# A hybrid decoder layer on one core: input projection by plain products, first weight sums of the MLP moved, final norm without GpSimd

## The chip, the cores and the metric

One core of a Trainium2 chip runs the whole layer as one program. The metric is device microseconds (us) of an execution, lower is better; comparisons are made between medians of several executions. The engines are TensorE (PE: matmuls; PEld its weight loads), VectorE (DVE), ScalarE (ACT), GpSimd (POOL) and SyncE (SP), which issues most DMAs. They run side by side, each through its own list of instructions in a fixed order, and wait for one another by semaphores.

## The reference

The input `x` is 1024 tokens by 1024 features in f32. One layer does, in f32:

```
h    = rmsnorm(x)
proj = h @ w_in                      # 1024 x 3080: u, v(gate MLP), q, k, v, gate, beta, decay
y_a  = gelu(u) * (tril(W_s) @ layernorm(gelu(v)) + b_s)        # chunks of 128 tokens, 4 groups
q, k, v = silu(causal depthwise conv of width 4)               # 4 heads x 128
y_b  = rmsnorm(gated delta rule(l2norm(q), l2norm(k), v)) * silu(gate)     # chunks of 64
x    = x + concat(y_a, y_b) @ w_out
x    = x + cross attention of rmsnorm(x) on 256 memory tokens  # 4 heads x 256
x    = x + relu(rmsnorm(x) @ w1)^2 @ w2                         # width 4096
out  = rmsnorm(x)
```

## The kernel before

Activations lie transposed in SBUF: features on the 128 partitions, tokens along the free axis, as eight blocks of features by two halves of 512 tokens. Every f32 product is made of three matmuls on rounded operands: an operand is split into a rounded part (`hi`, a CAST on ACT, L133) and the rest (`lo`, a subtraction on DVE, L134), and `mm3` issues hi x hi, hi x lo and lo x hi (L154 to L156). One product of a 128-row block of weights with 512 tokens over all 1024 features is 8 x 3 = 24 matmuls 128x512.

The program runs in stages: the gate MLP's `v` (0 to 54 us), the input projection with all that follows it per head (54 to 346 us), the delta rule (to some 550 us), the output projection, the memory attention (to some 780 us), w1 and w2 of the MLP, and the final norm.

**The input projection** works on 24 blocks of 128 output features; four of them (`v` of the gate MLP) are done by then. Blocks 0 and 1 are plain products (`u_block`, L385: 48 matmuls each). The other 18 go two at a time through `pair` (L491), which forms a 2 x 2 block product with 7 products instead of 8: each of the seven is 12 matmuls (`prod`, L507). What is saved is paid for with sums: of the weights, four for each pair, on GpSimd (L525 to L528), of the activations (`comb`, L421, on GpSimd, and the split operands that `quad` makes), and of the results: a PSUM bank that two results share is copied out by ACT (`save`, L517) before PE goes on adding into it, and the copy is added when a result is taken (L592 and others on DVE). A pair needs seven weight operands, split one by one just ahead of their product.

Results are taken by rows: `URow` (gelu), `GateRow` (silu, times a gain, stored to DRAM) and `ConvRow`: a convolution of width four along the tokens, one step on ACT (L604) and three on DVE (L606), then silu on ACT (L609). What follows a ConvRow on PE, the transposes to token order (L797) and the products k k^T and q k^T (L834), is put off by `post(..., PLAG)`: it comes when the counter that `boundary` (L473) raises after each product has gone `PLAG` further. L764 sums the log decays within chunks, of operands that GpSimd makes (L755). L716 is the mixing of the gate MLP, whose operands DVE normalises (L689). L574 takes a gate's result.

**The triangular inverse** of the delta rule, 31 steps of two DVE instructions that depend on one another (`inv_steps`, L892: L896 and L899), reads a matrix that is stored to DRAM (`u_d`) and loaded back (`ub_d` into `M`). Its result goes out as `ti_d` and comes back as `Tc`, which the first PE work of the delta rule reads (L1193). Until it is there PE runs `fill` work (products of the memory's keys and values, 128x256), in portions that `FILL` sets.

**The MLP's w1** (`w1_pair`, L1700) uses the same 2 x 2 scheme; its four sums of weights are on DVE (L1785 to L1788), its operands of activations are made by `early_quads` (in the attention's last stage) and `late_quads` (L1593). **The final norm** (`Norm`, L1888) sums squares on GpSimd (L1904), sums over partitions on PE (`rms_tok`, L179, columns of one), takes square root and reciprocal, spreads the result over the partitions (`rows`, L188) and multiplies: six of eight blocks on DVE (L1922), two by ACT and GpSimd (L1919, L1920).

A scheduler of the framework sets each engine's order, starting from that of the program text; on PE, from the delta rule on, due times written into the program set it. The orders printed below are those of the built programs.

## Time and profile before

| | |
|---|---|
| runs | 1437.39, 1436.9, 1433.65 us; median 1436.9 |
| profiled execution | 1440.11 us, span of its instructions 1438.1 us |
| mean granted TensorE clock | 0.975 of full speed |
| PE busy | 1379.9 us (96%) |
| DVE, ACT, POOL busy | 1054.4 (73%), 662.4 (46%), 223.6 us (16%) |

The profile's matmuls are pipelined, so that one is shown as busy while the next has begun: the rate of starts, not the busy share, tells how full PE is. A matmul 128x512 is shown with about 0.39 us but starts come about 0.23 us apart when nothing holds it up. The granted clock is 1.0 (2.4 GHz) or 0.5 (1.2 GHz) at any time; a mean between the two says which part of a stretch ran at the lower level.

### The profile page before, as it was taken

To read this page: it belongs to the slowest core of one execution; us is meant where nothing else is said; L and a number is where in the kernel's file an instruction comes from. 1 tells how busy PE (TensorE), PEld (TensorE's weight loads), DVE (VectorE), ACT (ScalarE), POOL (GpSimd) and SP (SyncE) were. 2 spreads that over 40 slices of the span, in tenths; PEclk is the share of its full clock that TensorE was granted. 3 is DMA by queue.
4 is the path that set the end of the run, shared out by engine and by line. 5 is a ranking of instruction groups with operands and counts; after the bars stand their busy time and mean duration, and the time that the engine had idled before them with its cause. 6 is when DMAs were issued, how large, how long until landed. Compare 5 with 4: busy or idle time off the path is not lost. (4 is left out here: it accounts for less than half of the span.)

```text
span 1438.1 us, 19110 instructions
## 1 busy us (share of the span) xinstructions
PE 1379.9 (96%) x6934; PEld 1147.7 (80%) x6934; DVE 1054.4 (73%) x1711; ACT 662.4 (46%) x1164; POOL 223.6 (16%) x182
## 2 busy tenths in 40 slices
PE   9989998979999999999999899999999999999996
PEld 8777777758998888888888788787787788888885
DVE  8797877789576656855547867766668997787775
ACT  7463565647455425744325444443344334333332
POOL 7551644440111102000000000000000000000024
PEclk9998999989999999999999999999999999999996
DMA  5102244538988878221300344444448664443203
GB/s 207 44 30 84 93 123 125 161 90 282 337 288 259 282 231 269 89 67 66 118 6 10 117 161 160 134 136 142 154 161 278 256 206 146 162 137 126 73 1 118
DMA packets 137008, 213.15 MB, mean 148 GB/s; under 512 B 22609, under 2 KB 73809, under 8 KB 136914
## 3 DMA queue, kind: packets, MB, share of 16 engines
q1 hardware_dynamic: 84352, 154.69, 33.6%
q10 hardware_dynamic: 52562, 57.25, 11.7%
q8 instruction: 54, 0.88, 0.2%
q14 instruction: 40, 0.33, 0.1%
HBM read 143.74 MB, written 68.16 MB: 147 GB/s over the span
## 5 line engine op out<-in xcount | busy, mean ns | idle before, releaser
L1904 POOL TENSOR_TENSOR rB<-rB,fq 128x256 f32<-128x256 f32 (+1 forms) x18 | 18.9, 1047 | 823.8 <-ACT fq L1902 823.3
L154 PE MATMUL mm<-A,wh 128*128 128x512 f32 (+1 forms) x368 | 138.0, 375 | 6.9 <-ACT F L517 4.4
L156 PE MATMUL mm<-A,wl 128*128 128x512 f32 (+1 forms) x368 | 135.0, 367 | 0.0
L133 ACT CAST wh<-raw 128x512 fp32r<-128x512 f32 (+1 forms) x110 | 83.1, 772 | 76.7 <-PE dn L155 24.0
L134 DVE TENSOR_TENSOR wl<-raw,wh 128x512 fp32r<-128x512 f32 (+1 forms) x103 | 97.2, 948 | 17.8 <-ACT wh L133 17.0
L155 PE MATMUL mm<-B,wh 128*128 128x512 f32 x240 | 97.7, 407 | 0.0
L154 PEld LDWEIGHTS mm<-A,wh 128*128 128x128 f32 x368 | 72.5, 197 | 18.5 <-ACT F L517 5.1
L156 PEld LDWEIGHTS mm<-A,wl 128*128 128x128 f32 x368 | 72.4, 197 | 10.7 <-DVE wl L134 0.5
L133 ACT CAST sp<-rw 128x1024 fp32r<-128x1024 f32 x36 | 37.5, 1051 | 92.6 <-issue 42.0
L1785 DVE TENSOR_TENSOR F<-raw 128x512 f32<-128x512 f32 x15 | 10.4, 693 | 70.5 <-DMA raw<-in_ffn_w_dram 70.5
L155 PE MATMUL mm<-A,wh 128*128 128x256 f32 (+1 forms) x192 | 61.9, 323 | 0.0
L154 PE MATMUL mm<-sp,sp 128*128 128x512 f32 (+1 forms) x152 | 58.1, 386 | 2.1 <-DVE A L1948 2.1
L155 PE MATMUL mm<-sp,sp 128*128 128x512 f32 (+1 forms) x152 | 58.5, 385 | 1.6 <-DVE sp L134 1.6
L156 PE MATMUL mm<-sp,sp 128*128 128x512 f32 (+1 forms) x152 | 58.3, 384 | 0.0
L155 PEld LDWEIGHTS mm<-B,wh 128*128 128x128 f32 x240 | 47.5, 198 | 9.5
L134 DVE TENSOR_TENSOR sp<-rw,sp 128x1024 fp32r<-128x1024 f32 x36 | 43.8, 1218 | 14.3 <-ACT sp L133 14.3
L1880 DVE TENSOR_TENSOR A<-mm,A 128x512 f32<-128x512 f32 x64 | 43.3, 684 | 8.5 <-PE mm L156 8.3
L154 PE MATMUL mm<-E,wh 128*128 128x512 f32 x116 | 45.4, 392 | 0.0
L155 PE MATMUL mm<-E,wh 128*128 128x512 f32 x116 | 45.1, 389 | 0.0
L1752 ACT ACTIVATE F<-F 128x512 f32<-128x512 f32 x31 | 19.6, 632 | 53.8 <-DVE F L1751 53.8
L1063 DVE TENSOR_TENSOR Y<-mm,Y 128x512 f32<-128x512 f32 x32 | 22.1, 690 | 29.5 <-PE mm L156 29.3
L1880 DVE TENSOR_TENSOR A<-dn,A 128x512 f32<-128x512 f32 x48 | 32.8, 686 | 13.7 <-PE dn L156 13.1
(688 smaller groups left out, 4309.6 us busy)
## 6 DMA issues: line engine op xcount, KB each, us to landing
raw<-in_ffn_w_dram SPq DMA_DIRECT2D x32, 512.0 KB, 4.6
raw<-in_w_in_dram SPq DMA_DIRECT2D x20, 512.0 KB, 3.9
rw<-hid_T_d SPq DMA_DIRECT2D x18, 512.0 KB, 3.3
hid_T_d<-F ACTq DMA_DIRECT2D x33, 256.0 KB, 2.1
rw<-hid_B_d SPq DMA_DIRECT2D x14, 512.0 KB, 3.3
Z<-in_ffn_w_dram SPq DMA_DIRECT2D x12, 512.0 KB, 4.1
rw<-in_ffn_w_dram SPq DMA_DIRECT2D x12, 512.0 KB, 5.0
hid_B_d<-F ACTq DMA_DIRECT2D x22, 256.0 KB, 2.4
```

The lines of the kernel that those rows point to most:

```text
L133: nc.scalar.copy(hi, src)
L134: (lo_eng or nc.vector).tensor_tensor(lo, src, hi.bitcast(F32), op=ALU.subtract)
L154: nc.tensor.matmul(out, wh, xh, start=start, stop=False, skip_group_check=more)
L155: nc.tensor.matmul(out, wh, xl, start=False, stop=False, skip_group_check=more)
L156: nc.tensor.matmul(out, wl, xh, start=False, stop=stop, skip_group_check=more)
L1063: nc.vector.tensor_tensor(a, ps[:], a, op=ALU.add)
L1752: nc.scalar.activation(o, o, AF.Square)
L1785: nc.vector.tensor_tensor(s1, a21, a22, op=ALU.add)
L1880: nc.vector.tensor_tensor(acc, ps[:], acc, op=ALU.add)
L1904: nc.gpsimd.tensor_tensor(self.sa, self.sa, self.sq, op=ALU.add)
```

## The change

The projection. The 18 blocks of the pairs become 18 plain rows; with blocks 0 and 1 there are 20, in the order `ORDER`, 48 matmuls each. `fetch_block` loads raw weights three to four blocks ahead into a ring of four buffers, `split_block` splits a whole block (128x1024) two blocks ahead into a ring of three. There are no sums of weights or activations, no saved banks; the scale 1/rms, which `before` put into the activations, is multiplied into each result on DVE when it is taken. `boundary` now comes after each 12 matmuls, and `PLAG` is 4. Between them, `hook` spreads small work over the rows: the gate MLP's statistics and mixing (`todo`), from row V1 on two steps of the inverse at each of the four hooks of a row, and the memory's norm in the last two rows.

The delta rule. The two `run_fill(1)` with the inverse's remainder go (it is done in the projection); `FILL` is 0.6 instead of 0.56.

The MLP. `first_sums` loads the first two blocks of w1, splits the first and makes the four sums of pair 0 during the last of the four groups of `attention_output`. The operand T3 is made of x11 and the difference that T2 already holds, T4 of x21 and the same: for each of four blocks one ACT and one DVE instruction fewer.

The final norm. The squares are summed on DVE (18 additions), all products are on DVE, and in the last quarter `rms_rows` takes the place of `rms_tok` and `rows`.

The core of the diff (names of tiles that only move, and the class bodies that lose the argument `plus`, left out):

```diff
-PLAG = 1
+PLAG = 4
 SLAG = 1
 MS, MN = 2, 5
-LOV = (3, 4)
-INV = (16, 31)
-FILL0, FILL = 5, 0.56
+INV = 2
+FILL0, FILL = 5, 0.6
+    def rms_rows(self, dst, parts):
+
+        ps = self.dn()
+        n = dst.shape[1]
+        for i, a in enumerate(parts):
+            self.nc.tensor.matmul(ps[:, :n], self.ones, a, start=i == 0, stop=i == len(parts) - 1)
+        self.nc.scalar.activation(dst, ps[:, :n], AF.Sqrt, bias=self.eps, scale=1.0 / D)
+        self.nc.vector.reciprocal(dst, dst)
+
...
-    def pair(rows_, saves, s1_tag, hook=None, los=()):
...
-        pa = e.mm()
-        w = slot()
-        e.split_copy(w[0], w[1], raw[0], eng(0))
-        wa, wb = ([v[:, 4 * b:4 * b + 4] for v in w] for b in range(2))
-        s1 = T(s1_tag, [P, 4, P])
-        nc.gpsimd.tensor_tensor(s1, a21, a22, op=ALU.add)
-        nc.gpsimd.tensor_tensor(a21, a11, a21, op=ALU.subtract)
-        nc.gpsimd.tensor_tensor(a11, s1, a11, op=ALU.subtract)
-        nc.gpsimd.tensor_tensor(a12, a12, a11, op=ALU.subtract)
-        prod(pa, wa, "11", True)
-        p1 = save(pa)
-        w = slot()
-        w2, w1 = split(w, 0, a11, 1), split(w, 1, s1, 2)
-        pb = e.mm()
-        prod(pb, wb, "21", True)
-        rows_[0].take(0, pb, p1)
-        prod(pa, w2, "T2", False)
-        u = save(pa)
-        w = slot()
-        w3, w4 = split(w, 0, a21, 3), split(w, 1, a12, 4)
-        pc = e.mm()
-        prod(pc, w1, "T1", True)
-        p5 = save(pc)
-        w5 = T("rB", [P, 4, P], F32R), T("rB2", [P, 4, P], F32R)
-        e.split_copy(*w5, a22, eng(5))
-        fetch_pair()
-        prod(pa, w3, "T3", False)
-        rows_[1].take(1, pa, p5)
-        prod(pc, w4, "22", False)
-        rows_[0].take(1, pc, u)
-        prod(pa, w5, "T4", False)
-        rows_[1].take(0, pa, None)
+    U, Q, K, V, G = ([n + i for i in range(4)] for n in (0, 8, 12, 16, 20))
+    ORDER = (U[0], U[1], G[0], K[0], Q[0], U[2], K[1], Q[1], U[3], K[2], Q[2], G[1], K[3], Q[3],
+             V[0], V[1], G[2], V[2], V[3], G[3])
+    ahead = deque(ORDER)
+    raws, ready = deque(), deque()
+    def fetch_block():
+        if ahead:
+            n = e.ring.get("wraw", 0)
+            e.ring["wraw"] = n + 1
+            tag = ("raw", "raw", "Z4", "Z5")[n % 4]
+            r = T(tag, [P, KT, P], F32, RAW if tag == "raw" else 1)
+            nc.sync.dma_start(r, t["w_in"][ahead.popleft()])
+            raws.append(r)
+    def split_block():
+        if raws:
+            n = e.ring.get("wsplit", 0)
+            e.ring["wsplit"] = n + 1
+            w = [T(t_, [P, KT, P], F32R, 2 if t_[0] == "w" else 1)
+                 for t_ in (("wh", "wl"), ("wh", "wl"), ("Z0", "Z1"))[n % 3]]
+            e.split_copy(*w, raws.popleft())
+            ready.append(w)
+        fetch_block()
+    def row(taker, hook=None):
+        wh, wl = ready.popleft()
+        for hf in range(2):
+            ps = e.mm()
+            for k in range(KT):
+                e.mm3(ps[:], wh[:, k], wl[:, k], *X[k][hf], k == 0, k == KT - 1)
+                if k == KT // 2 - 1:
+                    if hf == 0:
+                        split_block()
+                    if hook:
+                        hook()
+                    boundary()
+            taker.take(hf, ps)
+            if hook:
+                hook()
+            boundary()
         def take(self, hf, ps):
             pre = e.R("F0 F1 C18 C19", [P, 515])
-            if plus is None:
-                nc.scalar.copy(pre[:, 3:515], ps[:])
-            else:
-                nc.vector.tensor_tensor(pre[:, 3:515], ps[:], plus, op=ALU.add)
+            nc.vector.tensor_tensor(pre[:, 3:515], ps[:], rB[hf], op=ALU.mult)
...
+    def some_inv():
+        inv_steps(min(31, done[0] + INV))
+
+    row(v_row(0))
+    M = T("E2", [P, 32, 32])
+    nc.sync.dma_start(M, ub_d)
...
+    row(v_row(1), some_inv)
+    row(GateRow(2), some_inv)
+    row(v_row(2), some_inv)
+    row(v_row(3), lambda: (some_inv(), mem_norm()))
+    row(GateRow(3), lambda: (some_inv(), mem_norm()))
...
-    for n in INV:
-        run_fill(1)
-        inv_steps(n)
     inv_steps(31)
...
         if q == "T3":
-            nc.scalar.mul(b, x22, g2)
-            nc.vector.scalar_tensor_tensor(b, x12, n1, b, op0=ALU.mult, op1=ALU.add)
+            b = e.R("xr0 xr1 B3", [P, 512])
+            nc.vector.scalar_tensor_tensor(b, x11, n1, diff[j], op0=ALU.mult, op1=ALU.add)
         else:
-            hi, lo = XQ["T2"][j]
-            nc.vector.scalar_tensor_tensor(b, x21, g2, hi.bitcast(F32), op0=ALU.mult,
-                                           op1=ALU.subtract)
-            nc.vector.tensor_tensor(b, b, lo.bitcast(F32), op=ALU.subtract)
+            b = diff[j]
+            nc.vector.scalar_tensor_tensor(b, x21, g2, b, op0=ALU.mult, op1=ALU.subtract)
         put(q, j, b)
+    def first_sums():
+        for b in range(2):
+            r = T("raw", [P, KT, P], F32, RAW)
+            nc.sync.dma_start(r, t["ffn_w1"][b])
+            first_raw.append(r)
+        a11, a12, a21, a22 = (first_raw[b][:, 4 * i:4 * i + 4] for b in range(2) for i in range(2))
+        w = [T(t_, [P, KT, P], F32R, 2) for t_ in ("wh", "wl")]
+        e.split_copy(*w, first_raw[0])
+        yield
+        s1 = T("B1", [P, 4, P])
+        nc.vector.tensor_tensor(s1, a21, a22, op=ALU.add)
+        nc.vector.tensor_tensor(a21, a11, a21, op=ALU.subtract)
+        yield
+        nc.vector.tensor_tensor(a11, s1, a11, op=ALU.subtract)
+        nc.vector.tensor_tensor(a12, a12, a11, op=ALU.subtract)
+        first_raw.extend((w, s1))
+        yield
...
-                nc.gpsimd.tensor_tensor(self.sa, self.sa, self.sq, op=ALU.add)
+                nc.vector.tensor_tensor(self.sa, self.sa, self.sq, op=ALU.add)
...
+            if n0 > 0:
+                e.rms_rows(rb, [self.sa, self.sq])
...
-                    if m in (2, 5):
-                        nc.scalar.mul(acc, acc, g_of("norm_final", m))
-                        nc.gpsimd.tensor_tensor(ob[:, b], acc, rb, op=ALU.mult)
```

How the order changes, at three places.

PE in the projection. Before, rows around the first transposes of k of head 0 (`E_264`, half 0); the product that this half is taken from, `mm_1422`, ends at row 562:

```order
588 L154 MATMUL mm_1496<-A_150_785,wh_1416 128x512
589 L155 MATMUL mm_1496<-B_151_786,wh_1416 128x512
590 L156 MATMUL mm_1496<-A_150_785,wl_1417 128x512
591 L797 MATMUL dn_1471<-ident_86,E_264_1379 128x128 x4
592 L154 MATMUL mm_1381<-A_158_815,wh_1490 128x512
593 L155 MATMUL mm_1381<-B_159_816,wh_1490 128x512
594 L156 MATMUL mm_1381<-A_158_815,wl_1491 128x512
```

After, the same transposes (`E_183`); the product they come from, `mm_989`, ends at row 410:

```order
448 L153 MATMUL mm_1089<-A_44_261,wh_903 128x512
449 L154 MATMUL mm_1089<-B_45_262,wh_903 128x512
450 L155 MATMUL mm_1089<-A_44_261,wl_904 128x512
451 L701 MATMUL dn_1109<-ident_86,E_183_988 128x128 x4
452 L153 MATMUL mm_1089<-A_55_308,wh_903 128x512
453 L154 MATMUL mm_1089<-B_56_309,wh_903 128x512
454 L155 MATMUL mm_1089<-A_55_308,wl_904 128x512
```

The transposes moved back by half a product: before, 24 matmuls 128x512 of projection products (and four others) stand between the product and the transposes of its result; after, 36 (and four others).

DVE where the inverse begins. Before, in the row pair of v1 and gate 3 (L896, L899 the inverse; L592 takes a result, L606 the convolution, L134 a split):

```order
418 L899 TENSOR_TENSOR E_495_2643<-E_495_2643,E_496_2646 128x31
419 L896 TENSOR_TENSOR E_496_2646<-E_455_2414,E_495_2643 128x60
420 L899 TENSOR_TENSOR E_495_2643<-E_495_2643,E_496_2646 128x30x2
421 L896 TENSOR_TENSOR E_496_2646<-E_455_2414,E_495_2643 128x87
422 L899 TENSOR_TENSOR E_495_2643<-E_495_2643,E_496_2646 128x29x3
423 L896 TENSOR_TENSOR E_496_2646<-E_455_2414,E_495_2643 128x112
424 L899 TENSOR_TENSOR E_495_2643<-E_495_2643,E_496_2646 128x28x4
425 L896 TENSOR_TENSOR E_496_2646<-E_455_2414,E_495_2643 128x135
```

After, in row V1 (L812, L815 the inverse; L500 takes V1's two halves from `mm_2392` and `mm_2446`; L514 the convolution):

```order
316 L812 TENSOR_TENSOR E_381_2251<-E_402_2381,E_380_2248 128x31
317 L815 TENSOR_TENSOR E_380_2248<-E_380_2248,E_381_2251 128x31
318 L812 TENSOR_TENSOR E_381_2251<-E_402_2381,E_380_2248 128x60
319 L815 TENSOR_TENSOR E_380_2248<-E_380_2248,E_381_2251 128x30x2
320 L812 TENSOR_TENSOR E_381_2251<-E_402_2381,E_380_2248 128x87
321 L815 TENSOR_TENSOR E_380_2248<-E_380_2248,E_381_2251 128x29x3
322 L812 TENSOR_TENSOR E_381_2251<-E_402_2381,E_380_2248 128x112
323 L500 TENSOR_TENSOR C_413_2433<-mm_2392,rB_440 128x512
324 L815 TENSOR_TENSOR E_380_2248<-E_380_2248,E_381_2251 128x28x4
325 L506 COPY C_418_2483<-C_413_2433 128x3
326 L812 TENSOR_TENSOR E_381_2251<-E_402_2381,E_380_2248 128x135
327 L815 TENSOR_TENSOR E_380_2248<-E_380_2248,E_381_2251 128x27x5
```

Before, the first steps of the inverse stand in one run; after, one or two stand between the steps of each convolution, and the first of them stands ahead of the taking of V1's first half.

DVE at the start of w1. Before, the sums of pair 0 (L1785 to L1788) stand among the splits of its operands, behind the attention's last result (L1624):

```order
945 L1624 TENSOR_TENSOR A_1364_6832<-dn_7370,A_1364_6832 128x512
946 L134 TENSOR_TENSOR E_1450_7517<-F_1449_7514,E_1450_7517 128x512
947 L139 SCALAR_TENSOR_TENSOR E_1467_7592<-A_1362_6828,vec_84,E_1467_7592 128x512
948 L208 TENSOR_TENSOR rB_1367_6837<-rB_1367_6837,xr_1433_7396 128x512
949 L1590 SCALAR_TENSOR_TENSOR B_1436_7404<-F_1434_7399,ng_6834,B_1436_7404 128x512
950 L1785 TENSOR_TENSOR xr_1448_7505<-raw_7469 128x512
951 L1601 SCALAR_TENSOR_TENSOR xr_1455_7532<-A_1360_6824,ng_6834,xr_1455_7532 128x512
952 L134 TENSOR_TENSOR Y_1437_7407<-B_1436_7404,Y_1437_7407 128x512
953 L1786 TENSOR_TENSOR raw_7469<-raw_7467,raw_7469 128x512
954 L134 TENSOR_TENSOR Y_1447_7504<-xr_1448_7505,Y_1446_7503 128x512
955 L1787 TENSOR_TENSOR raw_7467<-xr_1448_7505,raw_7467 128x512
```

After, the sums (L1543 to L1547) and the first split stand around the attention's results (L1569), four of which are still to come behind them:

```order
815 L1569 TENSOR_TENSOR A_1256_6609<-mm_7001,A_1256_6609 128x512
816 L1543 TENSOR_TENSOR B_1319_7082<-raw_7035 128x512
817 L1507 TENSOR_TENSOR F_1335_7197<-A_1256_6609,A_1172_6189 128x512
818 L216 TENSOR_TENSOR rB_1263_6622<-rB_1263_6622,xr_1306_7027 128x512
819 L1544 TENSOR_TENSOR raw_7035<-raw_7033,raw_7035 128x512
820 L138 SCALAR_TENSOR_TENSOR Y_1336_7199<-F_1335_7197,vec_84,Y_1336_7199 128x512
821 L1546 TENSOR_TENSOR raw_7033<-B_1319_7082,raw_7033 128x512
822 L133 TENSOR_TENSOR wl_7365<-raw_7035,wh_7364 128x512
823 L1547 TENSOR_TENSOR raw_7033<-raw_7033 128x512
824 L1569 TENSOR_TENSOR A_1257_6611<-dn_7041,A_1257_6611 128x512
```

The four sums moved ahead of the attention's last four results.

## Rows read from the trace of the kernel before

**Rows 1.** The page: busy time by engine; granted clock in 40 slices.

```profile
PE 1379.9 (96%) x6934; PEld 1147.7 (80%) x6934; DVE 1054.4 (73%) x1711; ACT 662.4 (46%) x1164; POOL 223.6 (16%) x182
PEclk9998999989999999999999999999999999999996
```

**Rows 2.** Stretches: length, busy us by engine (count), clock, DMA share, GB/s.

```profile
54.00:345.90 291.90, 262.35 (x1210) 210.30 (x1209) 241.00 (x481) 154.15 (x351) 129.86 (x100) 0.94 0.37 107
345.90:382.00 36.10, 34.63 (x297) 33.70 (x295) 24.87 (x46) 22.81 (x32) 4.62 (x5) 0.95 1.06 348
780.00:822.00 42.00, 37.96 (x165) 30.08 (x164) 34.35 (x57) 24.13 (x43) 0.00 (x0) 0.92 0.29 101
1152.00:1224.00 72.00, 72.00 (x320) 59.61 (x319) 63.70 (x68) 29.76 (x30) 0.00 (x0) 1.00 0.54 182
1400.00:1438.00 38.00, 24.00 (x145) 22.80 (x144) 21.61 (x38) 11.68 (x29) 17.18 (x20) 0.70 0.32 111
```

**Rows 3.** Waits of PE, 54 to 346 us: total us, times, longest.

```profile
PE dn L797 <- ACT E L609: 16.6, 8, 5.0
PE mm L154 <- ACT F L517: 4.4, 1, 4.4
PE mm L154 <- ACT C L517: 2.8, 3, 1.7
PE mm L154 <- DVE C L574: 2.0, 1, 2.0
PE dn L716 <- DVE C L689: 1.6, 2, 1.1
PE dn L764 <- POOL C L755: 1.6, 2, 1.1
PE dn L764 <- POOL xr L755: 0.5, 1, 0.5
```

**Rows 4.** Timeline of PE at its longest wait there: start, duration, instruction.

```profile
292.77 0.39 PE L154 MATMUL mm<-A,wh 128*128 128x512 f32 x1
298.11 1.11 PE L797 MATMUL dn<-ident,E 128*128 128x128 f32 x4 [4.95 <-ACT E L609]
```

**Rows 5.** Groups on DVE and ACT there: busy us, mean ns | idle before.

```profile
L606 DVE SCALAR_TENSOR_TENSOR F<-F,vec,F 128x512 f32<-128x512 f32 x33 | 27.5, 842 | 0.1
L134 DVE TENSOR_TENSOR wl<-raw,wh 128x1024 fp32r<-128x1024 f32 x11 | 15.1, 1373 | 4.6 <-ACT wh L133 4.5
L592 DVE TENSOR_TENSOR F<-mm,C 128x512 f32<-128x512 f32 x12 | 8.2, 685 | 4.2 <-PE mm L156 2.7 <-ACT F L604 1.4
L835 DVE TENSOR_TENSOR E<-dn,E 128x512 f32<-128x512 f32 x16 | 10.9, 680 | 0.3 <-PE dn L834 0.3
L609 ACT ACTIVATE E<-F 128x512 f32<-128x512 f32 x21 | 13.3, 635 | 15.6 <-DVE F L606 15.5
```

**Rows 6.** The inverse on DVE; the load of its matrix (KB, us).

```profile
L896 DVE TENSOR_TENSOR E<-E,E 128x31 f32<-128x31 f32 (+15 forms) x31 | 13.6, 438 | 0.7
L899 DVE TENSOR_TENSOR E<-E,E 128x31 f32<-128x31 f32 (+15 forms) x31 | 12.4, 402 | 0.7
E<-u_d SPq DMA_DIRECT2D x1, 512.0 KB, 6.2
```

**Rows 7.** Waits of PE, 345 to 382 us (delta rule's start).

```profile
PE dn L1193 <- DMA Tc<-ti_d: 0.8, 1, 0.8
```

**Rows 8.** Waits of PE, 780 to 822 us (start of w1).

```profile
PE dn L154 <- ACT wh L133: 3.0, 1, 3.0
```

**Rows 9.** The end, 1400 to 1438 us: PE's waits; DVE timeline.

```profile
PE dn L179 <- POOL rB L1904: 3.6, 1, 3.6
PE mm L154 <- DVE A L1948: 2.1, 3, 1.6
1406.41 3.56 DVE L1922 SCALAR_TENSOR_TENSOR rw<-A,vec,fr 128x512 f32<-128x512 f32 x2
```

**Rows 10.** A reciprocal on DVE (timeline, 117 us).

```profile
116.76 0.34 DVE L653 RECIPROCAL E<-E 128x32 f32<-128x32 f32 x1
```

More of the change, by code (lines that the diff above doesn't have):

```diff
@@ L313, in hybrid @@
     z = [None] * NC
+    zz = {}
     def gv_step(ps, c, k):
@@ L854, in spill, with v_row, qk_rows @@
         return run
-    for h in range(NH):
+    def v_row(h):
+        vv = T(f"E{6 + h % 2}", [P, 2, 512])
+        vT = [vv[:, hf] for hf in range(2)]
+        return ConvRow(8 + h, vT, lambda hf: v_post(h, hf, vT))
+    def qk_rows(h):
         steps_ = decays(h)
```

223 lines of the change are left out of this document (78 added, 145 removed).

## Prediction

> **What bounds the kernel now.** Read first the share of PE and the clock: PE is shown busy for 1379.9 of 1438.1 us [rows 1], so at first sight there are 58 us to win. That share misleads, since a matmul is shown as busy while it waits for the one ahead; the count of starts is the better measure. A stretch that nothing disturbs holds 320 matmuls in 72 us at the full clock, 0.225 us for each 128x512 [rows 2]. The projection (54 to 345.9 us) ran at a mean clock of 0.94 [rows 2]; with two levels, 1.0 and 0.5, a mean 0.06 below full over 291.9 us is 17.5 us of work lost (35 us at the lower level). The page's slices have their lowest clock, 0.8, at 108 and 288 us, and 0.6 in the last one [rows 1]. Next the waits of PE by what released it: 29.5 us in the projection, 16.6 of them transposes that wait for a silu of a convolution, 7.2 the first matmul of a product that waits until ACT has copied a shared PSUM bank, 2.0 DVE taking a result, 1.6 and 2.1 others [rows 3]. The timeline shows what the longest is like: a matmul starts at 292.77, the transposes behind it only at 298.11, after a silu [rows 4]. Waits and clock together are 47 us in this stretch; from 1152 to 1224 us both are nil. So PE bounds everything, and what can be won is mostly in the first 350 us, some at the start of w1 and at the end.
>
> **The change, part by part.**
>
> *Work added.* A pair is 7 products of 12 matmuls, 84; two rows are 96. Nine pairs: 9 x 12 = 108 more matmuls 128x512, 108 x 0.225 = **+24.3 us**. That is certain, and on the path, as PE bounds.
>
> *Waits and clock of the projection.* The saves go, and the weight operands are ready two blocks ahead, so 7.2 us of the waits [rows 3] lose their cause. The transposes now stand 36 matmuls behind the product they come from, not 24: 8.1 us and not 5.4, at 0.225. What must fit in between for one half: taking 0.69, three convolution steps of 0.84, a step of ACT and the silu 0.64 [rows 5], some 4.6 to 5 us with the handovers, and another 1.4 where a split of 128x1024 stands between [rows 5]. By the old distance each hiccup of DVE reaches PE, by the new one 2 to 3 us of queue are swallowed. So the question is whether DVE keeps up. A row of q: two takings 1.4, six steps 5.1, a split 1.4, four products with the decays 2.7 [rows 5], small ones near 0.5: 11.1 us; a row of k is about as long, a row of u or gate 5 to 6. PE needs 48 x 0.225 = 10.8 for a row and near 1 for its transposes and small products. A round of k, q, u is 28 of DVE against 35 of PE: DVE fits, with peaks in the q rows. GpSimd's sums fall away, so PE's two waits for GpSimd's operands (2.1 us [rows 3]) shrink; I leave 1 us of them.
>
> The rows V are the hard ones. The inverse is 62 instructions in 26.0 us [rows 6], now two steps at each of four hooks, 26.0 x 8/31 = 6.7 us in a full row: a V row holds 1.4 + 5.1 + 1.4 + 6.7 = 14.6 us of DVE against 11.8 of PE. And its first step stands ahead of the taking of V1's first half on DVE, waits for the load of the matrix, which took 6.2 us once issued [rows 6], behind a store, behind the last products of q, which themselves now come later by the new distance. I put that load's landing some 9 us behind V0's end, DVE idle for 5 to 6 us, queued behind it V1's convolution, and PE 3 to 5 us at V1's transposes; V2 can lose a further 1 to 4. The mixing, done early, has no such wait.
>
> Residue: V rows 6, hiccups in the q rows 3, GpSimd and others 1, and about 3 for the clock after two or three longer waits: **13 us** left of 47, so −34. Both ends: 5 (only the wait for the load) and 27 (V rows as they were, half of the other waits and dips).
>
> *The start of the delta rule.* The inverse ends within the V rows, so the wait for its result, 0.8 us [rows 7], and the dip that goes with 0.95 over 36.1 us, 1.8 us [rows 2], should go; the fill work is moved, not changed. **−2** (−2.6 to +1: fills run out ahead of the first chunk).
>
> *The start of w1.* It holds a wait of 3.0 us of a product on a split of the second pair's weights [rows 8] and 0.08 x 42 = 3.4 us of clock [rows 2], 6.4 in all. Pair 0's sums and first split, 4 x 0.69 + 1.4 on DVE, leave the busiest 5 us of that engine, as do four subtractions; the buffers come free that much earlier, and so does the second pair's load. **−4.5** (−6.4 to +2: the sums stand ahead of the attention's last four results on DVE, and PE would wait for those).
>
> *The end.* GpSimd's share goes: two DVE products beside it took 3.56 us [rows 9], two of them elsewhere 2 x 0.84 at most [rows 5], and PE waited 2.1 us on the additions queued behind them [rows 9]: −2. The last chain waits 3.6 us on GpSimd's sum [rows 9]; an addition 128x256 is shorter on DVE, but DVE has 18 additions and six products more. The reciprocal of 128x256 is new: 0.34 us for 32 columns [rows 10] bounds it by 0.34 x 8 = 2.7 above, half of a 512-column addition, 0.35, below [rows 5]; I take 1.5, the middle. In return four transposing products, a copy and two column sums fall. I take **−1.5** (−4 to +2). The Trainium skill ("VectorE: DVE Perf Modes", "First, the fixed hardware budget") has the reciprocal run on an iterative divider with a repeat count of 8; at its clock of 0.96 GHz that would be an estimate of 2.1 us for 256 columns. By the same rule 32 columns would be 0.27 and the row shows 0.34 [rows 10], so the trace agrees; by it the end would be −0.9 instead of −1.5.
>
> *Sum.* +24.3 − 34 − 2 − 4.5 − 1.5 = −17.7 against the profiled execution of 1440.1, so 1422.4. That execution is 3.2 above the median of 1436.9; taken from the median, **1419**.
>
> **The rivals.**
>
> *Nearly every wait goes.* The residue is 5: 8 us better, 1411, and with w1 and the end at their better ends 1407; I take **1409**. For it: DVE has 20% in hand over most rows. Against: 14.6 against 11.8 in the V rows.
>
> *The inverse turns the V rows into DVE's.* Residue 27: +14, **1433**. It decides if the matrix lands more than some 12 us behind V0's end, so that V1 and V2 both wait. For it: 62 dependent instructions in line with the convolutions, and waits of up to 5.0 us at just such a place before [rows 3]. Against: only four of 20 rows have it.
>
> *Slower: DVE becomes the bound of all k, q and v rows.* The place is the convolution on DVE; the 24.3 us of matmuls are paid while the waits stay. To be slower by over 0.3% (4.3 us, about what a measurement of this kernel can tell from no change) the residue must exceed 34 + 13 − 24.3 + 8 + 4.3 = 35 us, so 12 rows must lose some 2 to 3 us each: a q row would have to take 14 us on DVE rather than 11.1. With a residue of 41 it would be **1447**. For it: DVE is busy for 241 of 291.9 us already [rows 2], and its queue is strictly in order, with takings behind products that wait for PE. Against: the sum of a round, and the removal of the activations' operands and bank additions from DVE.
>
> *It does nothing to the rest.* If the parts behind the projection bring nothing (they are off the path), 8 us of the gain fall and 1427 is left; that lies in the forecast's own range.
>
> **How the numbers follow.** Forecast (1411 to 1429, residue 8 to 20 with the other terms at either end) 0.55; nearly all waits go 0.17; V rows on DVE 0.16; slower 0.12. The range takes in the second and third: 1405 to 1434, leaving out the slower case and tails, near 0.2. Faster by over 0.3% means below 1432.6: the forecast, the first rival and half of the V-row case, 0.80. Within: the other half of it and a little of the slower case, 0.10; slower 0.10.
>
> **What the profile after would show.** Right: some 108 matmuls more, the projection about 12 us shorter from 54 us on, waits of PE on silu under 8 us and concentrated in the V rows, no wait on a saved bank, a clock of 0.98 or more there; no wait for the inverse's result; the wait at w1's second pair gone; no GpSimd beside DVE at the end. Wrong: DVE at 95% and more over whole rows of k and q, transposes waiting at each of them, the clock again near 0.94, PE waiting for DVE's takings, or new waits of the attention's last results on DVE. The forecast falls if the residue is over 27 or if the order of DVE makes one late load hold up a chain that I have counted as hidden.

## The result, and the profile after

The changed kernel takes 1416.4 us (median of four runs, 1415.7 to 1421.9), the kernel before 1435.3 (four runs): a ratio of 0.989, 95% interval 0.986 to 0.992. The forecast was 1419, so the time came out near it. The parts did not: two gains were larger than forecast, and a loss that no term held took most of the surplus away.

The page of the kernel after: span, busy time by engine, granted clock in 40 slices (it answers to [rows 1]).

```profile
span 1414.0 us, 19001 instructions
PE 1378.4 (97%) x7034; PEld 1154.2 (82%) x7034; DVE 1002.5 (71%) x1666; ACT 617.1 (44%) x1061; POOL 107.7 (8%) x100
PEclk9999999999999999999999999999999999999997
```

A hundred matmuls more, and PE is shown busy 1.5 us less: a matmul that waits behind another counts as busy, so this share says nothing of the gain. The slices at 0.8 in the projection are gone.

The stretches tell more. Columns: stretch, length, busy us of PE, PEld, DVE, ACT and POOL (count of each), granted clock, DMA share, GB/s. I cut the span at two events that both kernels have, the first fill matmul (the projection's end) and the last products with `Yc` (the last chunk's solve in the delta rule), and at a point 38 us ahead of the end. The projection of before is in [rows 2]; its other stretches:

```profile
345.90:524.00 178.10, 176.09 (x1460) 159.93 (x1459) 118.43 (x234) 89.08 (x148) 25.95 (x22) 0.99 0.91 289
524.00:1400.00 876.00, 864.53 (x3881) 711.03 (x3877) 628.48 (x910) 368.48 (x579) 21.11 (x14) 1.00 0.40 134
```

The same four stretches after:

```profile
54.00:325.70 271.70, 268.92 (x1332) 223.31 (x1331) 192.11 (x399) 118.00 (x268) 42.45 (x43) 0.99 0.43 124
325.70:512.20 186.50, 175.80 (x1449) 158.83 (x1447) 114.99 (x215) 86.55 (x143) 25.22 (x20) 0.98 0.83 252
512.20:1376.00 863.80, 858.04 (x3873) 708.11 (x3871) 626.66 (x910) 365.28 (x573) 12.57 (x9) 1.00 0.41 136
1376.00:1414.00 38.00, 22.76 (x142) 20.69 (x140) 26.25 (x59) 9.33 (x23) 0.00 (x0) 0.75 0.32 111
```

A cut 38 us ahead of the end gives the end the same length in both kernels, so the table goes on by events from the delta rule on: the last result of the attention that DVE takes (L1624, after the change L1569), and the first and the last result that `w2_group` takes (L1880, after it L1830).

| stretch | before | after | difference | forecast |
|---|---|---|---|---|
| projection, from 54 us | 291.9 | 271.7 | −20.2 | −9.7 |
| its end to the last products with `Yc` | 178.1 | 186.5 | +8.4 | −2 |
| to the attention's last result | 255.6 | 254.5 | −1.1 | none |
| to w2's first result (w1) | 328.1 | 318.1 | −10.0 | −4.5 |
| to w2's last result | 266.0 | 265.9 | −0.1 | none |
| to the end | 64.4 | 63.3 | −1.1 | −1.5 |
| sum (one execution of each) | | | −24.1 | −17.7 |

The profiled execution of before is 4.8 us above the median of its four runs, that of after 0.7 below: the 24.1 of the traces are some 19 in the medians, and differences of a few us between two traces can be scatter.

What PE waited for after (total us, times, longest). In the projection, in place of the seven rows and 29.5 us of [rows 3]:

```profile
PE dn L701 <- ACT E L517: 2.7, 1, 2.7
```

In the delta rule, 325 to 520 us (the two longest; [rows 7] showed 0.8 at its start, a wait that is gone):

```profile
PE dn L1206 <- ACT B L1200: 5.3, 1, 5.3
PE mm L154 <- DVE wl L133: 1.8, 1, 1.8
```

At the start of w1 (767 to 809 us, against [rows 8]) and in the last 38 us (against [rows 9]):

```profile
PE mm L153 <- ACT B L1678: 0.5, 1, 0.5
...
PE dn L187 <- DVE rB L1854: 3.5, 1, 3.5
PE mm L153 <- DVE A L1897: 2.6, 3, 1.0
```

So two places are open: why the projection lost nearly all of its 47 us of waits and clock, not 34, and where the delta rule's 8.4 us come from.

**The delta rule's new wait.** The timeline of after around it (start, duration, engine, instruction, idle before and its releaser; ACTq rows are DMA issues on ACT's queue):

```profile
442.12 0.42 DVE L907 TENSOR_TENSOR A<-mm,xr 128x256 f32<-128x256 f32 x1
442.82 0.58 ACT L750 COPY xr<-dn 128x512 f32<-128x512 f32 x1
449.72 0.69 DVE L485 TENSOR_TENSOR xr<-mm,rB 128x512 f32<-128x512 f32 x1 [3.32 <-DMA vt_d<-xr]
455.38 6.69 ACTq L947 DMA_DIRECT2D vw_d<-A  x4
465.71 0.58 ACT L1200 COPY B<-dn 128x512 f32<-128x512 f32 x1 [1.57 <-issue]
466.35 2.07 PE L1206 MATMUL dn<-B,B 128*128 128x128 f32 x8 [5.29 <-ACT B L1200]
```

L907 is the last reader of `rBm`, the spread norm of the memory. L750 copies a half of V2's values, L485 takes a gate's result: both are projection work, whose matmuls ended at 325, and they run some 120 us later. They write the buffer `xr1`, and `rBm` lies in `xr1`. The change had lengthened the ring `TR`, from which the values, the gates and the operands of the log decays are taken, by that buffer; the diff has it among the tiles that only move:

```diff
-    TR = "C24 C25 xr0"
+    TR = "C24 C25 xr0 xr1"
```

My reading: a row of V2 takes `xr1` from the ring, must wait until the memory's keys are scaled at 442, and hands its lateness on: the store from `xr1` holds L485 and DVE for 3.3 us, the load of these values comes late, and stores and copies on ACT pile up ahead of L1200, which a chunk's chain needs. The experiment e_rbm settles whether this buffer is the cause; the links in between are read from this timeline alone.

**The projection's old waits.** First what ACT waited for there in the kernel before (54 to 346 us, the longest total of its list):

```profile
ACT wh L133 <- POOL raw L527: 18.1, 5, 5.7
```

An instance of it, timeline of before: GpSimd's third weight sum (L527) behind another product of its own, ACT, and the transposes on PE.

```profile
196.98 1.49 POOL L822 TENSOR_TENSOR E<-E,E 128x512 f32<-128x512 f32 x1
198.43 1.30 POOL L527 TENSOR_TENSOR raw<-C,raw 128x512 f32<-128x512 f32 x1
199.76 0.62 ACT L133 CAST wh<-raw 128x512 fp32r<-128x512 f32 x1 [3.33 <-POOL raw L527]
200.29 0.73 ACT L604 ACTIVATE F<-C,vec 128x512 f32<-128x512 f32 x1
205.20 0.63 ACT L609 ACTIVATE E<-F 128x512 f32<-128x512 f32 x1 [1.14 <-DVE F L606]
205.88 0.66 PE L797 MATMUL dn<-ident,E 128*128 128x128 f32 x4 [3.01 <-ACT E L609]
```

GpSimd's third sum ends at 199.73; the CAST that splits it stands ahead of the convolution's step L604 in ACT's queue, which is in order, so L604 starts some 3 us late, the silu follows, and PE waits 3.0 us for it. This wait, which [rows 3] put down to a silu, began with an addition on GpSimd. The two other long ones of the k and q rows, and ACT's wait for GpSimd in the same stretches (210 to 250 and 250 to 290 us):

```profile
237.32 1.01 PE L797 MATMUL dn<-ident,E 128*128 128x128 f32 x4 [2.77 <-ACT E L609]
267.96 0.66 PE L797 MATMUL dn<-ident,E 128*128 128x128 f32 x4 [1.57 <-ACT E L609]
```

```profile
ACT wh L133 <- POOL raw L527: 3.1, 1, 3.1
...
ACT wh L133 <- POOL raw L527: 2.3, 1, 2.3
```

Each time PE waits a little less than ACT did: 3.0, 2.8 and 1.6 against 3.3, 3.1 and 2.3. ACT's two other waits of the five, 3.7 and 5.7 us (they end at 118 and 153 us), are not followed by such a wait of PE, so 8.7 of the 18.1 us stand ahead of 7.3 us of silu waits. After 290 us, in the V rows, ACT has no such wait, and PE still waits three times for a silu there, at 298 [rows 4], 310 and 337, for 8.3 us together. At 298 the three convolution steps stand on DVE between splits and last 0.74, 1.21 and 1.21 us, GpSimd's additions beside them. So the 16.6 us are two parts, 7.3 and 8.3, with causes of their own (the last 0.9 are two short waits). After the change there are no weight sums that ACT could wait for.

### The profile page after: what moved, and what is told of

It reads as the page before. It is cut to its first block, busy times and chain, and to the rows that moved or that the text cites. A ratio compares the mean times of both kernels' runs of the same rounds, so it can differ in the third digit from the quotient of the medians.

```text
span 1414.0 us, 19001 instructions
## 1 busy us (share of the span) xinstructions
PE 1378.4 (97%) x7034; PEld 1154.2 (82%) x7034; DVE 1002.5 (71%) x1666; ACT 617.1 (44%) x1061; POOL 107.7 (8%) x100
## 5 line engine op out<-in xcount | busy, mean ns | idle before, releaser
L153 PE MATMUL mm<-A,wh 128*128 128x512 f32 (+1 forms) x416 | 153.6, 369 | 0.0
L155 PE MATMUL mm<-A,wl 128*128 128x512 f32 (+1 forms) x416 | 149.2, 359 | 0.0
L154 PE MATMUL mm<-B,wh 128*128 128x512 f32 x288 | 112.9, 392 | 0.0
L155 PEld LDWEIGHTS mm<-A,wl 128*128 128x128 f32 x416 | 78.9, 190 | 12.1 <-DVE wl L133 0.2
L153 PEld LDWEIGHTS mm<-A,wh 128*128 128x128 f32 x416 | 79.0, 190 | 11.1
L132 ACT CAST wh<-raw 128x512 fp32r<-128x512 f32 (+1 forms) x79 | 63.0, 808 | 56.2 <-PE dn L154 23.4
L133 DVE TENSOR_TENSOR wl<-raw,wh 128x512 fp32r<-128x512 f32 (+1 forms) x78 | 74.2, 953 | 18.4 <-ACT wh L132 17.7
L154 PEld LDWEIGHTS mm<-B,wh 128*128 128x128 f32 x288 | 54.6, 190 | 10.6
L1735 DVE TENSOR_TENSOR F<-raw 128x512 f32<-128x512 f32 x15 | 10.4, 691 | 57.6 <-DMA raw<-in_ffn_w_dram 57.6
L1830 DVE TENSOR_TENSOR A<-mm,A 128x512 f32<-128x512 f32 x64 | 43.3, 684 | 8.5 <-PE mm L155 8.3
L154 PE MATMUL mm<-B,Z 128*128 128x512 f32 x124 | 48.4, 390 | 0.0
L1830 DVE TENSOR_TENSOR A<-dn,A 128x512 f32<-128x512 f32 x48 | 32.7, 685 | 13.7 <-PE dn L155 13.1
L155 PE MATMUL mm<-E,wl 128*128 128x512 f32 x108 | 42.1, 390 | 0.0
```

Source lines behind the costliest of these rows:

```text
L132: nc.scalar.copy(hi, src)
L133: (lo_eng or nc.vector).tensor_tensor(lo, src, hi.bitcast(F32), op=ALU.subtract)
L153: nc.tensor.matmul(out, wh, xh, start=start, stop=False, skip_group_check=more)
L154: nc.tensor.matmul(out, wh, xl, start=False, stop=False, skip_group_check=more)
L155: nc.tensor.matmul(out, wl, xh, start=False, stop=stop, skip_group_check=more)
L1735: nc.vector.tensor_tensor(s1, a21, a22, op=ALU.add)
```

## Experiments

Twelve kernels, in three sets on one chip each; the kernel before was run with each set (medians 1433.3, 1434.7, 1433.1). The kernel e_rbm is the base of seven of them.

| kernel | median us | ratio to before, 95% |
|---|---|---|
| e_again: after, unaltered | 1419.6 | 0.991 (0.988 to 0.993) |
| e_rbm: after, `rBm` in a buffer of its own | 1403.7 | 0.980 (0.977 to 0.983) |
| e_mlp_old: after, MLP as before | 1424.1 | 0.993 (0.991 to 0.995) |
| e_norm_old: after, final norm as before | 1418.1 | 0.989 (0.986 to 0.992) |
| e_before_far: before, PLAG 3 | 1448.0 | 1.008 (1.006 to 1.011) |
| e_near: e_rbm, PLAG 3 | 1410.9 | 0.983 (0.981 to 0.985) |
| e_inv_late: e_rbm, INV 0 | 1406.2 | 0.980 (0.978 to 0.982) |
| e_ops_old: e_rbm, operands T2 to T4 as before | 1406.2 | 0.980 (0.978 to 0.982) |
| e_pool_back: e_rbm, idle additions on GpSimd | 1411.6 | 0.984 (0.982 to 0.987) |
| e_split_one: e_rbm, weights split one block ahead | 1405.7 | 0.980 (0.978 to 0.983) |
| e_fill_56: e_rbm, FILL 0.56 | 1406.6 | 0.982 (0.980 to 0.984) |
| e_best_norm_old: e_rbm, final norm as before | 1404.3 | 0.980 (0.978 to 0.982) |

**e_again**, the kernel after without an edit, as a measure for its set.

> The changed kernel unaltered, as the base for the others on this chip. Every theory expects it near 1416 us (1415.7 to 1421.9 so far) and 0.986 to 0.9915 of the kernel before.

1419.6 (1417.3 to 1421.6), within the range of the first four runs. In its trace the projection lasts 274.7 us, with three waits of 4.0 us together, and the delta stretch 188.2, against 271.7 and 186.5 in the table: so much the same program scatters.

**e_rbm**, one line:

```diff
-    rBm = T("xr1", [P, NM])
+    rBm = small(NM)
```

> The changed kernel, with the row of the memory's norm (rBm) in a part of the tile E0 instead of the buffer xr1. Theory: the change put xr1 into the ring in which gate and value results of the projection stand, while rBm holds that buffer until the last of the memory's keys and values (DVE, some 442 us); so one value result is copied only at 442.8 us and the last gate result taken only at 449.7 us, their stores and the loads behind them come late, and PE waits 2.07 us at 455.4 and 5.5 us at 460.9, with 6.8 us at half the clock behind it. It expects these waits gone, the stretch from the last projection product to the attention 7 to 10 us shorter, and 1406 to 1409 us. Rival: the waits come from less fill work before the first chunk (168 matmuls 128x256 instead of some 228) and FILL 0.6, the late results being harmless; it expects the waits to stay and 1416 us.

1403.7: 15.8 us below e_again in the same set. Its windows of the projection and the delta stretch, its waits of PE from 54 to 520 us, and one row of its timeline on ACT:

```profile
54.00:324.50 270.50, 268.08 (x1333) 222.23 (x1332) 191.59 (x401) 118.39 (x269) 41.78 (x43) 1.00 0.44 126
324.50:499.70 175.20, 173.06 (x1447) 157.02 (x1446) 116.16 (x215) 83.48 (x140) 25.02 (x20) 1.00 0.84 266
```

```profile
PE dn L701 <- ACT E L517: 2.3, 4, 0.7
PE dn L1149 <- ACT B L1139: 1.0, 1, 1.0
PE dn L1128 <- DVE X L1122: 0.8, 1, 0.8
PE dn L1206 <- ACT B L1200: 0.4, 1, 0.4
```

```profile
308.90 0.59 ACT L750 COPY xr<-dn 128x512 f32<-128x512 f32 x1
```

The last fence is the copy L750 that ran at 442.82 before this edit. The delta stretch is 175.2 us against 186.5 (188.2 in e_again), the wait of 5.3 on L1200 is 0.4, and the clock is full. The buffer is the cause; without it the stretch is 2.9 us shorter than before's 178.1, near the −2 of the forecast. The median lies below the 1406 to 1409 expected, since the projection is shorter too: 270.5 us against 271.7 and 274.7. Its waits are hardly fewer, four of at most 0.7 and 2.3 in all in place of one of 2.7 (three of 4.0 in e_again), but the mean clock is 1.00 instead of 0.99. What the buffer does to that stretch was not followed. This version beats both kernels.

**e_mlp_old**: `first_sums` out, T2 to T4 as before the change.

```diff
-        sums = first_sums()
...
-            if g == 3:
-                next(sums)
```

> The changed kernel with w1's start as before: first two blocks, split and sums of pair 0 behind the attention, T3 and T4 as before. Theory: the part is worth what the traces show between the attention's last result and the first result of w2, 10 us (8.8 and 9.5 us of PE's lost time in the two stretches against 1.0 and 7.0); it expects the 3.0 us wait on the split of pair 1 and a dip of the clock back, and 1424 to 1427 us. Rival (the prediction's size): 4.5 us, 1421. A second rival: the waits went because the stage started in another state (an engine less behind), and the part itself brings under 2 us: 1417.

1424.1: by the medians 4.5 us above e_again, the size of the rival that stands for the prediction, and the intervals of the two overlap. The stage tells more: the waits of PE at 770 to 815 us, and the window from the attention's last result to w2's first, with after's own beside it:

```profile
PE dn L153 <- ACT wh L132: 3.0, 1, 3.0
```

```profile
766.80:1094.20 327.40, 318.60 (x1383) 259.14 (x1383) 239.87 (x366) 140.65 (x232) 0.00 (x0) 0.98 0.45 152
```

```profile
766.70:1084.80 318.10, 314.17 (x1391) 257.14 (x1390) 234.69 (x359) 137.12 (x225) 0.00 (x0) 1.00 0.47 156
```

The wait of 3.0 is back, and over the first 42 us of the window the clock is 0.92 as in before, 1.00 in after. The stretch is 327.4 us long, as before's 328.1, against 318.1 in after and 318.7 in e_again. The eleven traces with `first_sums` have 317.9 to 320.4 there, the three without it 327.0 to 328.1, so the part is worth some 9 us in its stage. The profiled executions of e_mlp_old and e_again differ by 3.8 us only, since the first reaches the attention's last result 4.2 us earlier (766.8 us against 771.0, 766.7 in after), in stages that the edit leaves alone. Whether the medians' 4.5 has the same reason is not shown.

**e_norm_old** and **e_best_norm_old**: the final norm as before, in after and in e_rbm.

```diff
-                nc.vector.tensor_tensor(self.sa, self.sa, self.sq, op=ALU.add)
+                nc.gpsimd.tensor_tensor(self.sa, self.sa, self.sq, op=ALU.add)
...
-            if n0 > 0:
-                e.rms_rows(rb, [self.sa, self.sq])
```

> The changed kernel with the final norm as before (squares summed by GpSimd, two of eight products on ACT and GpSimd, column sums and transposing products in the last quarter). Theory: the part is worth what the traces show behind the last full product of w2, 1 to 2 us; it expects 1417.5 us, DVE's products beside GpSimd at 1.8 us again, and PE waiting for GpSimd at the end. Rival: the new long reciprocal and the additions on DVE eat the gain, 1416 or a little under. Both are near what the measurement can tell; the profiles' last 38 us decide.

> The changed kernel with rBm moved (1403.7 us), and the final norm as before. With the norm's old form beside the new one on another base (1418.1 against 1419.6 and 1416.4 us) nothing was decided; from the last full product of w2 to the end those profiles had 36.0 us with the old norm and 37.1 with the new. Theory: the norm's part brings nothing or costs up to 1.5 us: 1402 to 1404 us. Rival (the prediction): it gains 1.5 us: 1405 us.

1418.1 against 1419.6 and 1416.4 for after; 1404.3 against 1403.7 for e_rbm, in different sets with ratios 0.9797 and 0.9798. The new norm brings nothing that can be measured; with intervals of 0.2% to either side, 3 us, the 1.5 us forecast are not excluded either. The waits of PE in the last 39 us of e_best_norm_old:

```profile
PE dn L178 <- POOL rB L1845: 3.4, 1, 3.4
PE mm L153 <- DVE A L1889: 2.1, 3, 1.6
PE dn L187 <- DVE r L170: 0.6, 1, 0.6
```

6.1 us, and 7.6 in e_norm_old and 6.3 in before, all with the old norm; with the new one 6.1 in after and 6.2 in e_rbm. The last chain waits about as long for DVE's sum as it did for GpSimd's.

**e_before_far**: the kernel before with the transposes put off by two products of 12 matmuls more, by the program's text as far as in after.

```diff
-PLAG = 1
+PLAG = 3
```

> The kernel before with one number changed: PLAG 3 instead of 1, so that 36 matmuls or more of projection products stand between a result and its transposes, as in the changed kernel, and not 24. Theory: the distance alone takes away most of the 16.6 us that PE waited for a silu, and with it most of the 17.5 us lost to the clock in the projection; it expects 1412 to 1420 us, so nearly the whole gain of the change without 108 more matmuls. Rival: the pair scheme itself (DVE behind with seven operands and bank additions, ACT copying banks) makes results late and keeps the dips; it expects 1428 to 1436 us.

Slower than before by 0.8%, 1448.0. Waits of PE, 54 to 354 us (the three longest), and ACT's wait for GpSimd:

```profile
PE dn L834 <- ACT E L776: 10.2, 3, 3.4
PE mm L154 <- ACT C L517: 6.4, 8, 1.7
PE dn L797 <- ACT E L609: 5.5, 5, 1.7
```

```profile
ACT wh L133 <- POOL raw L527: 18.3, 5, 5.7
```

That is slower than either side expected. The silu waits fell from 16.6 us to 5.5, as the distance should have them, and ACT still stood 18.3 us behind GpSimd. New waits took the place: the largest, three of 3.4 us, are at the products k k^T (L834), which read nothing of the decays' exp (L776, on ACT); by the program's text what they wait for is a PSUM bank that the exp reads. At the first of them, 182.6 to 186.0 us, ACT is not behind GpSimd: it has no gap between sums of squares (L803), a table load of 1.28 us and the exps. So the longer distance also set other work in PE's way, and the run does not part the two. It shows that distance alone, in the kernel before, moves the waits and gains nothing.

**e_near**: e_rbm with 24 matmuls between product and transposes, as before had them.

```diff
-PLAG = 4
+PLAG = 3
```

> The changed kernel with rBm moved (1403.7 us), and PLAG 3 instead of 4: 24 matmuls between a result and its transposes, 5.4 us, as in the kernel before. Theory: a half row needs 4.6 to 5 us on DVE and ACT and 1.4 more with a split in between, so waits of 0.5 to 2 us come back at most of the 24 halves, and dips of the clock with them; it expects 1411 to 1422 us. Rival: with splits two blocks ahead and no sums DVE takes results so promptly that 24 are enough; it expects 1403 to 1407 us.

1410.9, by the ratios 4.4 us above e_rbm; the intervals overlap, but the projection of its trace is longer by as much, 275.0 us against 270.5. One wait in the whole projection, and the split on DVE ahead of it:

```profile
PE dn L701 <- ACT E L517: 3.9, 1, 3.9
```

```profile
268.44 1.29 DVE L133 TENSOR_TENSOR Z<-raw,Z 128x1024 fp32r<-128x1024 f32 x1 [3.99 <-ACT Z L132]
```

It is in row V0, at 269 us, with a fall of the clock behind it, and it has no step of the inverse at its head. A step of the memory's norm on ACT (L851) waits 3.2 us for the memory's load, the CAST of a weight block stands behind it, DVE's split waits 4.0 us for that CAST, and V0's convolution stands behind the split. The k and q rows have no wait at the old distance. So the step of the prediction "By the old distance each hiccup of DVE reaches PE, by the new one 2 to 3 us of queue are swallowed" does not hold for those rows: the hiccups themselves went. The longer distance is worth some 4.4 us, in a V row.

**e_split_one**: one block split ahead in place of two.

```diff
-    for _ in range(2):
+    for _ in range(1):
         split_block()
```

> The changed kernel with rBm moved (1403.7 us), and the weights split one block ahead of their product instead of two. Theory: a block lasts 10.8 us on PE and a split 2.3 us on ACT and DVE, so one block ahead is enough and the third pair of buffers brings nothing: 1403 to 1406 us. Rival: DVE's queue before a split is at times longer than a row, and PE waits for weights at several rows: 1408 to 1418 us.

1405.7, no difference to e_rbm beyond the intervals; one wait of 0.7 us on a silu. The depth of the splits is not the reason either.

**e_pool_back**: two additions 128x512 on GpSimd behind each split, on raw weights that nobody reads again. They put work on GpSimd beside DVE; nothing waits for their result except the buffer's next load, but what GpSimd does next stands behind them.

```diff
+            for b in range(2):
+                nc.gpsimd.tensor_tensor(r[:, 4 * b:4 * b + 4], r[:, 4 * b:4 * b + 4],
+                                        r[:, 4 * b:4 * b + 4], op=ALU.add)
```

> The changed kernel with rBm moved (1403.7 us), and two GpSimd additions of 128x512 on each raw block of w_in behind its split: GpSimd's load of the weight sums before (four for a pair of rows) is there again, its result used by nobody. Theory: GpSimd beside DVE lengthened DVE's convolution steps (0.84 us in the kernel before), which made results late; so they grow again from some 0.75 us and PE's waits for a silu come back in part: 1408 to 1416 us. Rival: DVE has so much in hand in the rows that longer steps do not reach PE: 1403 to 1406 us.

1411.6, by the ratios 6.5 us above e_rbm; the intervals just overlap, and the projection of its trace, of its slowest run, is 10.8 us longer. Waits of PE and the two groups of convolution steps on DVE (54 to 335 us; by the buffer that a row's operand lies in, half of the rows each; busy us, mean ns | idle before):

```profile
PE dn L705 <- ACT E L521: 8.3, 3, 4.3
```

```profile
L518 DVE SCALAR_TENSOR_TENSOR F<-C,vec,F 128x512 f32<-128x512 f32 x36 | 33.7, 936 | 3.7 <-ACT F L516 2.9
L518 DVE SCALAR_TENSOR_TENSOR F<-F,vec,F 128x512 f32<-128x512 f32 x36 | 29.8, 826 | 6.8 <-ACT F L516 6.2
```

Work on GpSimd lengthens DVE's steps: 936 and 826 ns, 787 and 802 in e_rbm. One instance in a q row, three steps while GpSimd added from 252.2 to 255.1 us (2.33 us where nothing ran beside them):

```profile
252.04 3.64 DVE L518 SCALAR_TENSOR_TENSOR F<-C,vec,F 128x512 f32<-128x512 f32 x3
```

The k and q rows have five such instances of 3.6 us and no wait of PE. The three waits are at 272, 290 and 309 us, all in the V rows. Ahead of those at 290 and 309 DVE has steps of the inverse and of the convolution that are up to three times as long as their like (1.2 and 1.5 us), with GpSimd's additions beside them. The longest, 4.3 at 272, is another chain. As in e_near, ACT waited for the memory's load first (5.7 us); then its norm step stood behind a GpSimd addition (L856) that was queued behind two of the added ones, and the silu that PE needed came next on ACT, at 275.70:

```profile
272.09 2.48 POOL L451 TENSOR_TENSOR raw<-raw 128x512 f32<-128x512 f32 x2
275.28 0.42 ACT L855 ACTIVATE E<-E 128x256 f32<-128x256 f32 x1 [2.23 <-POOL E L856]
```

So GpSimd's load brings waits back in the V rows, as many us as in before, partly by longer steps on a full DVE and partly by holding up ACT. In the k and q rows, where ACT waits for no result of GpSimd, the longer steps cost PE nothing.

**e_inv_late**: no steps of the inverse at the hooks (`INV = 0`), meant to leave them for the projection's end.

> The changed kernel with rBm moved (1403.7 us), and no step of the inverse in the rows V: all 31 come in one run on DVE when the projection is done. Theory: 62 instructions of 26.0 us, a store and a load follow the projection, of which the fill work ahead of the first chunk (168 matmuls 128x256, 20.2 us) covers the larger part; PE then waits 8 to 14 us for the inverse, a dip of the clock behind it: 1411 to 1419 us. Rival: DVE is free in the rows V, starts the inverse while they still run, and the fill work covers the rest: 1402 to 1406 us.

Inconclusive: 1406.2, and the 31 steps (L812) ran from 270.6 to 307.3 us, in e_rbm from 270.3 to 307.1. The scheduler put them at the same place without hooks, so the experiment tells nothing of what the inverse costs there, only that the hooks are not what places it.

**e_ops_old**: e_rbm, T2 to T4 formed as before; `first_sums` stays.

```diff
-            nc.vector.scalar_tensor_tensor(diff[j], diff[j], n1, b, op0=ALU.mult, op1=ALU.add)
-            put(q, j, diff[j])
+            nc.vector.scalar_tensor_tensor(b, diff[j], n1, b, op0=ALU.mult, op1=ALU.add)
+            put(q, j, b)
```

> The changed kernel with rBm moved (1403.7 us), and T2, T3, T4 of w1's operands made as before (one more ACT and one more DVE instruction for each of four blocks); the first sums of weights stay in the attention. It tells apart which half of the MLP's part carried its 8 us. Theory: the sums and the split do, since they freed the buffers for pair 1; it expects 1403 to 1406 us. Rival: DVE's queue as a whole was the limit at the start of w1, and four instructions of 0.7 us count like the others; it expects 1406 to 1410 us.

1406.2, no difference beyond the intervals, and the stage to w2's first result is 319.8 us, 319.0 in e_rbm. The eight instructions saved are off the path; what is left as the source of the MLP part's 9 us is the early load, split and sums, which were not taken out alone.

**e_fill_56**: e_rbm with `FILL` 0.56, as before had it.

> The changed kernel with rBm moved (1403.7 us), and FILL 0.56 as before. It is the rest of the change in the delta rule. Theory: with the inverse early the rate of fill work between the chunks matters little: within 1.5 us of 1403.7. Rival: the higher rate brings the last fills, and so the stage's end, nearer: slower by 2 to 6 us.

1406.6, 2.4 us above e_rbm by the ratios and 2.9 by the medians, not beyond the intervals. It stays undecided, and small.

## Why the prediction was right, and where it was not

The total was right because errors of opposite sign met, which is luck: by the traces 10.5 us too little for the projection and 5.5 too little for w1's stretch, 1.2 in stretches without a term, against 10.4 of loss in the delta stretch and 0.4 too much for the end. With the one buffer moved, e_rbm is at 1403.7, below the whole range of 1405 to 1434.

*Work added, +24.3.* Right. Between 54 us and the projection's end the trace has 960 matmuls 128x512 against 852; that stretch of e_rbm, with them and 2.3 us of wait, is 270.5 us at a clock of 1.00.

*Waits and clock of the projection: 13 us left of 47.* Mis-sized: the rows of after leave 2.7 of wait and, with 0.99 over 271.7 us, about 2.7 of clock, 5.4; by the lengths (24.3 more work and 20.2 less time) only 2.5 are left, and the 3 us between the two are not located. Of the residue's parts, "hiccups in the q rows 3" and "GpSimd and others 1" came to nothing, and the V rows lost 2.7 with the fall of the clock behind it, rather than 6 and 3. The step that failed is the one that had DVE's hiccups behind the silu waits, and the distance to swallow them. ACT's own waits, which I had not read, name another cause for the k and q rows: GpSimd's sums, with the convolution queued behind them on ACT. The runs bound it: distance does not bring the loss back in the k and q rows of after (e_near) and gains nothing in before (e_before_far), the depth of the splits does nothing (e_split_one), longer steps on DVE cost PE nothing in those rows (e_pool_back), and where ACT stands behind GpSimd for over 2 us again, in e_pool_back at 275 us, PE waits for the silu behind it. ACT behind GpSimd as the head of the chain fits all of them and three instances of the trace; a kernel before with only these sums taken off GpSimd was not run, so it is not shown by itself.

*V rows.* The price was too high, the place right in the main: every long wait of PE for a silu after the change (2.7 in after, 3.9 in e_near, 8.3 in e_pool_back) is in a V row. The late matrix, the prediction's reason for 3 to 5 us at V1's transposes, cost less: in after it landed at 268.5 us, 6.4 behind V0's last product and not 9, DVE was idle 2.1 us for it and not 5 to 6, and V1's transposes did not wait. The wait of 2.7 is at V2's first half (302 us), behind a DVE that goes through steps of the inverse without a gap; there the count of 14.6 us of DVE against 11.8 of PE fits. That ACT's queue can hold up a V row (e_near), and that GpSimd's load lengthens DVE's steps there and would be gone, was not in it.

*The start of the delta rule, −2.* Right as to what it speaks of: the wait for `Tc` [rows 7] is gone, and e_rbm's stretch is 2.9 shorter. But the sum stopped there. The line `TR` had been read as a tile that only moves; its users and the last reader of the tile that shares the buffer were not compared. It cost 8.4 + 2.9 = 11.3 us in this stretch by the traces of after and e_rbm, 13.0 by those of e_again and e_rbm, and the projection is 4.2 longer in e_again's: together 17.2, where the medians of the two are 15.8 apart. The prediction's last sentence had the kind of mishap ("one late load hold up a chain that I have counted as hidden"), with no place and no price.

*The start of w1, −4.5.* Right in mechanism, too small by the stage: 10.0 us between the attention's last result and w2's first, of which the change of the MLP is some 9 (the total of e_mlp_old alone would give 4.5). I had taken 6.4 for all that could be won and left some of it, while the smaller waits went too.

*The end, −1.5.* 1.1 us between two traces, and nothing that the runs can tell from none. The two DVE products beside GpSimd, 3.56 us [rows 9], did become shorter, but DVE's own work in the stretch grew from 21.6 us [rows 2] to 26.3, PE's wait on the last sum stayed (3.6 [rows 9], 3.5 after), the one on the additions went from 2.1 to 2.6. The reciprocal was guessed at 1.5 us; timeline of DVE after:

```profile
1405.42 1.75 DVE L189 RECIPROCAL fr<-fr 128x256 f32<-128x256 f32 x1 [2.40 <-ACT fr L188]
```

1.75, 6.8 ns for a column. That is less than the estimate of 2.1 us worked out in the prediction from the repeat count in the Trainium skill ("VectorE: DVE Perf Modes", "First, the fixed hardware budget"); the measurement decides. From 32 columns (0.34 [rows 10]) to 256 the time grows by 6.3 ns a column, not by the 8.3 of that estimate, so the agreement at 32 columns was not one of the rule.

*The rivals.* "Nearly every wait goes" was what the projection did, with a residue of 2.5 to 5.4; without the shared buffer the kernel is at 1403.7, 5 below its 1409. "The inverse turns the V rows into DVE's" fell (residue 5.4 at most, not 27). "DVE becomes the bound" fell: DVE is busy 192 of 271.7 us, 71%, where it had been 241 of 291.9 [rows 2], 83%. "It does nothing to the rest" is wrong for w1 and cannot be excluded for the end.

## What to carry to other kernels

When PE waits for an activation, follow that engine's own waits one step further before you price a remedy: here ACT's queue stood behind a sum on GpSimd, which the waits of PE alone do not tell. When a change adds a buffer to a ring, list who else uses that buffer and when its last reader runs; one shared tile cost over 11 us here, a line of the diff that computes nothing. And compare stage by stage even when the total fits, between the same events in both kernels: a right total can be two errors.

## What the runs showed of the hardware

Two additions on GpSimd (128x512) lengthened three convolution steps on DVE beside them from 2.33 to 3.64 us, though DVE needed nothing from GpSimd; over all rows the two groups of steps went from 787 to 936 ns and from 802 to 826 (e_rbm, e_pool_back). And four DMA issues in a row on ACT's queue span 6.69 us in after, where the late values are stored and loaded at the same time, while one issue of that line lasts 0.36 to 1.30 us; in e_rbm no group of four at that line spans more than 3.67. ACT ran nothing else from 455.8 to 462.1 us, and the copy that PE's chain needed came at 465.7. What the rest of the 6.69 us was spent on is not shown.
